# Chunk 0 of all 13 first blocks before any other chunk, other visit ranges, another root, two more raw buffers, and one background for all four modulation sums

## The chip, the cores and the metric

The kernel runs on one core of a Trainium2 chip. The metric is the device time of one execution in microseconds, the median of the runs. Before the change it is 1599.73 us (three runs, 1598.8 to 1605.01).

## What is computed

One layer of an autoregressive decoder, for 256 tokens of width 2048, all in f32. The conditioning vector c gives six modulation vectors, each silu(c) times a 2048 x 2048 part of w_ada. Two residual sub-layers follow; `mixing_sublayer` is one wide projection, three token mixers with gates, and an output projection.

```python
mod = silu(c) @ w_ada + b_ada
shift1, scale1, gate1, shift2, scale2, gate2 = split(mod, 6)
h = rms_norm(x, norm1_gain) * (1 + scale1) + shift1
x = x + gate1 * mixing_sublayer(h, w_in, ..., w_out)      # w_in: 15 blocks of 512 columns, then 3 x 2048 gates
h = rms_norm(x, norm2_gain) * (1 + scale2) + shift2
g, u = split(h @ w_ffn_in, 2)
x = x + gate2 * ((silu(g) * u) @ w_ffn_out)
```

The mixers are a stick-breaking attention, a dilated attention in three groups and a gated linear attention. Their inputs come from the first 13 blocks of w_in's columns (0 to 12).

## The kernel before

**Products.** Every f32 weight is split into two parts that TensorE takes at full pace: ACT casts the raw tile to `whi` (L167, or L245 in the Strassen pairs), and DVE subtracts to get `wlo` (L168, L231). Activations H are split likewise. A product of one 128x512 weight chunk with two row tiles of 128 tokens is six matmuls (`mm3`, lines 175 to 177; line 662 in the first stretch). `load_weights` (L142) loads two chunks at a time, 512 KB, into one of four rotating `raw` buffers (L155, L156). SP issues all loads, in the order of its own queue; a load waits until the buffer it goes to is free, and all loads behind it in the queue wait too.

**w_in.** H of chunk k (16 chunks of 128 rows) needs shift1 and scale1 of these rows. They come from column sums ("MACs"): DVE multiplies a 128x1024 tile of the transposed w_ada with silu(c), which lies broadcast in the tile "ada" (cB), and adds along the row (`column_mac`, L430). One chunk takes four MACs and four loads of 512 KB. Since not all of H is there at first, blocks 0 to 12 are visited several times: `first_chunks` does chunk 0 of blocks 1 to 4 and chunks 0 to 2 of blocks 5 to 8, then each of VISITS does a range of chunks for a group of blocks (X, Y or Z), and LAST does chunks 10 to 15 of each block. Between visits the partial sums go from PSUM to SBUF (`evict`, L623, on ACT) and are seeded again (L611, ACT). In `first_chunks` the instructions of TensorE, ACT and DVE keep the order in which they are written (`in_order`); elsewhere a scheduler with priorities (`prio`, `issue_after`) orders each engine.

**The first microseconds.** k_vec is loaded first, then x in four parts. silu(c) is spread over the partitions (16 matmuls, L379). Squares of x are summed by matmuls with ones (L549), `root_of` makes the reciprocal root (L556 to L562), and the columns of shift1 and scale1 for chunk 0 come from matmuls (`by_pe`, L705) and DVE steps (`by_dve`, L714) that meet in `part`. `keep_warm` adds matmuls that compute nothing (WARM).

**Background.** The four other vectors are also made by MACs: 128 of them, spread over the kernel by a generator that `tick` advances at state["rate"] for each two chunks. `background` (L1163) does shift2, gate1 and scale2; `gate2_bg` (L1438) is a second generator, started at the first block of w_out. `flush` at FFN unit 2 forces out all that is left.

**Later stages.** Blocks 13 and 14, the gate blocks, three gate pairs, `y_block` 0 to 3 (w_br), four blocks of w_out (the fourth in two passes, one per row tile), w_ffn_in: units 0 and 1 plain, units 2 to 10 as Strassen-like pairs (`fast_products`, L264), and w_ffn_out. `load_pair` (L218) takes its raw tile from the four `raw` buffers and from `more_raws`, which in the FFN are the tiles AR1 and "ada". The counter state["raws"] says which comes next; it is set to 0 ahead of the FFN, and only `load_pair` advances it.

Of the kernel before, what the change touches and what calls it, by code (L numbers as in the profile page):

```python
# [10 lines left out]
F32 = mybir.dt.float32  # L11
# [6 lines left out]
P = 128  # L18
# [67 lines left out]
def trunk(ctx: ExitStack, tc: tile.TileContext, I, out):  # L86
# [57 lines left out]

    def load_weights(src, k0, k1, b, spare=(), ahead=True, late=None):
# [72 lines left out]
    def load_pair(src, p, b0, b1, fast, tags):  # L218


        def raw_at(b):
            more_raws = state.get("more_raws", ())
            i = state["raws"] = (state.get("raws", -1) + 1) % (4 + len(more_raws))
            raw = S(more_raws[i], [P, 2, NB]) if i < len(more_raws) else wp.tile([P, 2, NB], F32, tag="raw", name=nm("raw"))
            nc.sync.dma_start(raw, src[b, :, 2 * p : 2 * p + 2, :])
            return raw
# [214 lines left out]
    FIRST_TAGS = ("OS0", "OS1", "OS2", "OD", "T4", "T5", "A9", "A10", "A11", "A12", "A8", "A7")  # L441
# [109 lines left out]
    def root_of(sums):  # L551


        act = nc.scalar.activation
        v, y, z, r = (x for x in S("X0", [P, 4, T]).rearrange("p a t -> a p t"))
        act(v, sums, AF.Identity, bias=eps_c[:, 0:1], scale=1.0 / D)  # L556
# [68 lines left out]
    def first_chunks():  # L625
# [37 lines left out]

        nc.sync.dma_start(vec, I["k_vec"])
        for j in range(3):
            nc.sync.dma_start(xT[j], I["x_t"][:, 4 * j : 4 * j + 4, :])
# [4 lines left out]
        for a in (0, 2):
            nc.sync.dma_start(rows[3][:, a : a + 2], I["ada_0"][:, 12 + a : 14 + a, :])
        load_two(0, 1, True)
        for b in (3, 5, 7):
            load_two(0, b)
        for k in (1, 2):
            load_mods(k)
            if k == 1:
                for b in (5, 7):
                    load_two(k, b)  # L680

        with in_order():
# [26 lines left out]
            def by_dve(k):  # L709
                row, c = rows[k // 4][:, k % 4, :], csil[:, k : k + 1]  # L710
                if k == 2:
                    nc.vector.tensor_scalar(part, row, c, None, op0=ALU.mult)
                else:
                    nc.vector.scalar_tensor_tensor(part, row, c, part, op0=ALU.mult, op1=ALU.add)  # L714

            for k in (0, 1, 4, 5, 8, 9, 12, 13):
                by_pe(rows[k // 4][:, k % 4, :], k)
            for k in (2, 3, 6, 7):
                by_dve(k)
            r = state["root"] = root_of(sums)  # L720
# [3 lines left out]
            for k in (10, 11):
                by_dve(k)
            for k in (14, 15):
                by_pe(rows[3][:, k % 4, :], k)
            by_pe(part, None, True)
# [12 lines left out]
            xs = {b: [acc_bank() if b < 3 else misc_bank([P, NB]) for _ in range(NT)] for b in BLOCKS_X}
            for b in BLOCKS_X:
                products(0, b, xs[b], True, True)
                if b % 2:
                    cast_two(0, b + 4)
                    lows(0, b + 4)
                evict(b, xs[b])
# [940 lines left out]
```

## Time and profile before

| | before |
|---|---|
| median of three runs | 1599.73 us |
| profiled execution | 1599.51 us |
| its span, first to last instruction | 1597.7 us |
| mean granted TensorE clock | 0.993 |
| TensorE busy | 1557.0 us, 97% |
| VectorE (DVE) busy | 1374.7 us, 86% |
| ScalarE (ACT) busy | 920.0 us, 58% |
| first product with w_in starts | 19.60 us |
| w_out's first product starts | 775.1 us |
| longest wait of TensorE | 13.0 us |

A row of the timeline has the start in us, the duration in us, the engine, the line of the kernel, the operation, output<-inputs, the shape and a count of like instructions drawn together; in brackets stands how long the engine was idle ahead of it and what it waited for. PE is TensorE, PEld its weight load, SPq the issue of a DMA by SyncE. A row of waits has the waiting line, the awaited line, the sum in us, the number and the longest. A row of windows has the stretch and its length, each engine's busy time with its instructions, the granted clock of TensorE (1.00 is full), the share of time in which the 16 DMA engines were busy, and GB/s. Durations of matmuls overlap; their pace is read from their starts.

### The profile page before, as it was taken

What the parts mean: (1) busy time and instruction counts of PE and PEld (TensorE: products, weight loads), DVE (VectorE), ACT (ScalarE), POOL (GpSimd) and SP (SyncE); (2) the same over time, 40 slices, a digit from 0 to 9 for tenths busy, and PEclk for the clock granted to TensorE, in tenths of its full rate; (3) what the DMA queues carried; (4) which work ended last, traced back from release to release, by engine and by line L of the source; (5) the groups of instructions that cost most, each with busy time, mean ns of one, the idle gap of its engine ahead of it and who ended that gap; (6) DMA issues with size and microseconds to landing.
All of it is one profiled execution on the core that took longest, in us unless ns stands there. A gap on an engine that the chain in (4) does not pass through costs nothing.

```text
span 1597.7 us, 20015 instructions
## 1 busy us (share of the span) xinstructions
PE 1557.0 (97%) x7067; PEld 1279.6 (80%) x7067; DVE 1374.7 (86%) x1837; ACT 920.0 (58%) x1292; POOL 5.0 (0%) x11
## 2 busy tenths in 40 slices
PE   8999999999999999999999996999999999999998
PEld 6778778888888778888887875888888888888887
DVE  7987866987978999978888876999999999789886
ACT  5787777866756454444445533555655655455553
POOL 0000000000000000000000000000000000000000
PEclk9999999999999999999999998999999999999999
DMA  9999986766787778889997784665656566656764
GB/s 349 340 335 320 353 298 215 253 189 222 256 296 272 255 245 271 295 269 333 338 332 277 262 300 140 208 212 190 201 190 213 196 196 222 201 185 188 231 205 140
DMA packets 113380, 399.20 MB, mean 250 GB/s; under 512 B 12512, under 2 KB 13408, under 8 KB 113280
## 3 DMA queue, kind: packets, MB, share of 16 engines
q1 hardware_dynamic: 112704, 395.84, 73.2%
q0 software_dynamic: 576, 2.10, 0.3%
q8 instruction: 55, 0.90, 0.2%
q14 instruction: 45, 0.37, 0.1%
HBM read 393.69 MB, written 4.19 MB: 249 GB/s over the span
## 4 chain that ended last, share of the span: by engine, by line
PE 71%; DVE 12%; DMA 8%; ACT 4%; issue 4%; SPq 0%; DVEq 0%; ACTq 0%
PE acc L176 15%; PE acc L177 14%; PE acc L175 14%; PE misc L176 8%; PE misc L177 8%; PE misc L175 8%; DVE wlo L168 3%; DMA raw<-w_ffn_in 2%; ACT whi L167 2%; DVE wlo L231 1%; DMA AR<-ada_t 1%; DVE A L231 1%; DMA raw<-w_in 1%; DMA raw<-w_out 1%; DMA raw<-w_br_gla 1%
## 5 line engine op out<-in xcount | busy, mean ns | idle before, releaser
L168 DVE TENSOR_TENSOR wlo<-raw,whi 128x1024 fp32r<-128x1024 f32 (+1 forms) x265 | 311.7, 1185 | 106.9 <-ACT whi L167 106.1
L167 ACT CAST whi<-raw 128x1024 fp32r<-128x1024 f32 (+1 forms) x265 | 269.2, 1022 | 221.5 <-PE acc L177 92.5
L176 PE MATMUL acc<-wlo,H 128*128 128x512 f32 x854 | 334.6, 392 | 4.6 <-DVE wlo L168 3.0
L175 PE MATMUL acc<-whi,H 128*128 128x512 f32 x854 | 332.0, 392 | 4.3 <-ACT whi L167 2.4
L177 PE MATMUL acc<-whi,H 128*128 128x512 f32 x854 | 333.1, 390 | 0.1
L176 PEld LDWEIGHTS acc<-wlo,H 128*128 128x128 f32 x854 | 160.5, 188 | 41.7 <-DVE wlo L168 7.8
L175 PEld LDWEIGHTS acc<-whi,H 128*128 128x128 f32 x854 | 160.4, 188 | 37.9 <-ACT whi L167 2.8
L177 PEld LDWEIGHTS acc<-whi,H 128*128 128x128 f32 x854 | 160.3, 188 | 33.3 <-DVE H L1422 0.5
L245 ACT CAST whi<-raw 128x1024 fp32r<-128x1024 f32 (+1 forms) x126 | 121.1, 973 | 63.6 <-PE acc L177 25.6
L231 DVE TENSOR_TENSOR wlo<-raw,whi 128x1024 fp32r<-128x1024 f32 (+1 forms) x126 | 139.7, 1122 | 17.6 <-ACT whi L245 16.3
L176 PE MATMUL misc<-wlo,H 128*128 128x512 f32 (+1 forms) x297 | 116.0, 390 | 1.2 <-DVE wlo L168 1.1
L177 PE MATMUL misc<-whi,H 128*128 128x512 f32 (+1 forms) x297 | 115.3, 389 | 0.0
L175 PE MATMUL misc<-whi,H 128*128 128x512 f32 (+1 forms) x297 | 113.2, 389 | 0.9 <-ACT whi L167 0.9
L177 PE MATMUL acc<-whi,A 128*128 128x512 f32 x221 | 86.2, 390 | 0.0
L176 PE MATMUL acc<-wlo,A 128*128 128x512 f32 x210 | 82.1, 391 | 2.1 <-DVE wlo L168 2.1
L175 PE MATMUL acc<-whi,A 128*128 128x512 f32 x210 | 82.0, 391 | 1.0 <-ACT whi L167 1.0
L176 PEld LDWEIGHTS misc<-wlo,H 128*128 128x128 f32 x297 | 55.8, 188 | 15.6 <-DVE wlo L168 4.0
L175 PEld LDWEIGHTS misc<-whi,H 128*128 128x128 f32 x297 | 55.7, 188 | 13.0 <-ACT whi L167 1.4
L177 PEld LDWEIGHTS misc<-whi,H 128*128 128x128 f32 x297 | 55.7, 188 | 11.5 <-DVE H L591 0.4
L231 DVE TENSOR_TENSOR A<-raw,A 128x1024 fp32r<-128x1024 f32 (+2 forms) x58 | 55.5, 962 | 3.1 <-ACT A L245 2.7
L245 ACT CAST A<-raw 128x1024 fp32r<-128x1024 f32 (+1 forms) x35 | 34.4, 989 | 31.5 <-DMA raw<-w_in 10.2
L623 ACT COPY A<-acc 128x512 f32<-128x512 f32 x64 | 37.0, 585 | 22.8 <-PE acc L177 20.1
(711 smaller groups left out, 3145.2 us busy)
## 6 DMA issues: line engine op xcount, KB each, us to landing
raw<-w_in SPq DMA_DIRECT2D x191, 512.0 KB, 5.1
raw<-w_ffn_in SPq DMA_DIRECT2D x135, 512.0 KB, 4.8
raw<-w_ffn_out SPq DMA_DIRECT2D x73, 512.0 KB, 4.3
AR<-ada_t SPq DMA_DIRECT2D x61, 512.0 KB, 5.6
raw<-w_out SPq DMA_DIRECT2D x32, 512.0 KB, 5.6
OS<-ada_t SPq DMA_DIRECT2D x26, 512.0 KB, 7.3
KD<-ada_t SPq DMA_DIRECT2D x24, 512.0 KB, 5.9
T<-ada_t SPq DMA_DIRECT2D x23, 512.0 KB, 7.5
```

Of the source, the lines that this page charges most:

```text
L167: state["cast"] = nc.scalar.copy(hi[:, :n, :], raw[:, :n, :])
L168: state["split"] = nc.vector.tensor_tensor(lo[:, :n, :], raw[:, :n, :], hi[:, :n, :].bitcast(F32), op=ALU.subtract)
L175: nc.tensor.matmul(ps, lh, rh, start=start, stop=False, skip_group_check=seeded)
L176: nc.tensor.matmul(ps, lh, rl, start=False, stop=False, skip_group_check=seeded)
L177: state["mm"] = nc.tensor.matmul(ps, ll, rh, start=False, stop=stop, skip_group_check=seeded)
L231: done = nc.vector.tensor_tensor(dst, x, y, op=ALU.subtract)
L245: nc.scalar.copy(hi[:, :n, :], src)
L623: nc.scalar.copy(A[b][:, t, :], pss[t])
```

## The change

1. In `first_chunks`, x's first quarter is loaded ahead of k_vec, and the rows of w_ada for chunk 0 between x's parts. The squares, warming matmuls and mods are interleaved in another order.
2. `root_of` drops one ACT step: Ln reads the sums directly, and DVE makes v beside it. DVE steps of `part` stand between the root's steps.
3. Chunk 0 is done for all 13 blocks first, in the order 1, 2, 3, 4, 9, 10, 11, 12, 0, 5 to 8; then chunks 1 and 2 of blocks 5 to 8. All but blocks 5 to 8 are evicted after chunk 0.
4. VISITS and LAST have other ranges: the last visits now begin at chunk 9 (X), 11 (Y) or 10 (Z).
5. `load_weights` takes X1 and X2 as two more raw buffers, from the first visit until gate_block(0, 1).
6. One background makes shift2, scale2, gate1 and gate2 in this order. It starts at the first of the last visits with rate 0.7 (before, blocks 0 to 4 there had rate 0), and later rates are lower. `gate2_bg` is gone.
7. state["raws"] starts the FFN at 1 and is also advanced by `load_weights`, which there has no extra buffers, so that each call counts in fours.
8. `normed` and the sums of h are issued behind the latest split.

```diff
-RATE_IN, RATE_MID, RATE_GATES, RATE_PAIRS, RATE_Y, RATE_LAST = 0.8, 0.6, 0.65, (0.42, 0.25, 0.25), 0.55, 0.75
+RATE_IN, RATE_MID, RATE_GATES, RATE_PAIRS, RATE_Y, RATE_LAST = 0.7, 0.6, 0.6, (0.25, 0.2, 0.2), 0.55, 0.75
-RATES_OP, RATES_FFN = (0.95, 0.9, 0.0), (0.95, 0.95, 0.85, 0.8)
+RATES_OP, RATES_FFN = (0.9, 0.7, 0.0), (0.75, 0.9, 0.7, 0.6)
-WARM = (8, 2, 1, 3)
+WARM = (8, 2, 2, 2, 2, 3)
+RATE_FIRST = 0.7
-VISITS = ((BLOCKS_Z, 0, 3, 3, 5), (BLOCKS_X, 1, 5, 5, 7), (BLOCKS_Y, 3, 6, 7, 8), (BLOCKS_Z, 3, 7, 8, 10),
-          (BLOCKS_X, 5, 10, 10, 12), (BLOCKS_Y, 6, 10, 12, 14), (BLOCKS_Z, 7, 10, 14, 16))
-LAST = (10, 16)
+VISITS = ((BLOCKS_X, 1, 4, 4, 5), (BLOCKS_Z, 1, 5, 5, 7), (BLOCKS_Y, 3, 7, 7, 9), (BLOCKS_X, 4, 9, 9, 11),
+          (BLOCKS_Y, 7, 11, 11, 13), (BLOCKS_Z, 5, 10, 13, 16))
+LAST = {b: (k0, KC) for bs, k0 in ((BLOCKS_X, 9), (BLOCKS_Y, 11), (BLOCKS_Z, 10)) for b in bs}
...
+    def raw_tile(more):
+        i = state["raws"] = (state.get("raws", -1) + 1) % (4 + len(more))
+        return S(more[i], [P, 2, NB]) if i < len(more) else wp.tile([P, 2, NB], F32, tag="raw", name=nm("raw"))
...
-                raw = wp.tile([P, step, w], F32, tag="raw", name=nm("raw"))
+                raw = raw_tile(state.get("load_raws", ()))
...
-            more_raws = state.get("more_raws", ())
-            i = state["raws"] = (state.get("raws", -1) + 1) % (4 + len(more_raws))
-            raw = S(more_raws[i], [P, 2, NB]) if i < len(more_raws) else wp.tile([P, 2, NB], F32, tag="raw", name=nm("raw"))
+            raw = raw_tile(state.get("more_raws", ()))
...
-    def root_of(sums):
+    def root_of(sums, between):
...
-        act(v, sums, AF.Identity, bias=eps_c[:, 0:1], scale=1.0 / D)
-        act(y, v, AF.Ln)
+        first = xT[0][:, 0, :]
+        act(y, sums, AF.Ln, bias=eps_c[:, 0:1], scale=1.0 / D)
+        nc.vector.tensor_scalar(v, sums, 1.0 / D, EPS, op0=ALU.mult, op1=ALU.add)
         act(y, y, AF.Exp, scale=-0.5)
         act(z, y, AF.Square)
+        between()
+        nc.vector.tensor_tensor(first, first, y, op=ALU.mult)
         nc.vector.tensor_mul(z, z, v)
         nc.vector.tensor_scalar(z, z, -0.5, 1.5, op0=ALU.mult, op1=ALU.add)
+        nc.vector.tensor_tensor(first, first, z, op=ALU.mult)
...
+        x_in(0, 0, 4)
         nc.sync.dma_start(vec, I["k_vec"])
...
+            squares(0, "X1", 0, 4, sums)
+            keep_warm(WARM[2])
+            squares(1, "X2", 0, 4, sums)
+            keep_warm(WARM[3])
+            squares(2, "AR0", 0, 4, sums)
+            on_pe(0, 1)
+            on_dve(2, 3)
+            for a in (0, 2):
+                squares(3, "AR1", a, a + 2, sums)
+            r = state["root"] = root_of(sums, lambda: on_dve(6, 7))
+            on_pe(4, 5)
+            keep_warm(WARM[4])
+            on_pe(8, 9)
             for dst, ps in state["spreads"]:
                 nc.scalar.copy(dst, ps)
-            normed(r, 0, 1)
...
+            on_dve(10, 11)
+            on_pe(12, 13)
+            by_pe(part, None)
+            on_pe(14)
+            by_pe(rows[3][:, 3, :], 15, True)
...
+    state["load_raws"] = ("X1", "X2")
...
     def background():
-        for seg in (SEG_SHIFT2, SEG_GATE1, SEG_SCALE2):
...
+        for seg in (SEG_SHIFT2, SEG_SCALE2, SEG_GATE1, SEG_GATE2):
...
+    state["rate"] = RATE_FIRST
...
+    state["load_raws"] = ()
     gate_block(0, 1, turns)
...
-    bg.append(gate2_bg())
...
-    state["raws"] = state["tiles"] = 0
+    state["raws"], state["tiles"] = 1, 0
```

Three places in the order. First SP's queue at the entry of the FFN's pairs, before: ada_t is w_ada transposed (a MAC's load), L156 a plain weight load, L225 a raw of a pair.

```order
L423 DMA A_1749_8140<-ada_t 128x1024
L423 DMA KC_8170<-ada_t 128x1024
L156 DMA raw_8234<-w_ffn_in 128x1024
L156 DMA raw_8240<-w_ffn_in 128x1024
L156 DMA raw_8246<-w_ffn_in 128x1024
...
L225 DMA raw_8449<-w_ffn_in 128x1024
L225 DMA AR_1825_8457<-w_ffn_in 128x1024
L225 DMA raw_8455<-w_ffn_in 128x1024
L225 DMA ada_8367<-w_ffn_in 128x1024
L225 DMA ada_8417<-w_ffn_in 128x1024
```

And the same place now (the lines of the new file are L426, L161 and L228):

```order
L161 DMA raw_8088<-w_ffn_in 128x1024
L426 DMA KC_7973<-ada_t 128x1024
L161 DMA raw_8094<-w_ffn_in 128x1024
L161 DMA raw_8100<-w_ffn_in 128x1024
L161 DMA raw_8106<-w_ffn_in 128x1024
L161 DMA raw_8112<-w_ffn_in 128x1024
L161 DMA raw_8234<-w_ffn_in 128x1024
L228 DMA ada_8408<-w_ffn_in 128x1024
L161 DMA raw_8240<-w_ffn_in 128x1024
```

The tile ada_8367, the first raw of the first pair, stood behind nine other raws of pairs. Now the load into "ada" stands among the plain loads, and the last load of a MAC a few rows ahead of it.

Second, DVE at the eight splits of w_out's first block (`wlo`; L1333 and L1334 are sums of the last y block, L336 a split of transposed y), before:

```order
L168 TENSOR_TENSOR wlo_6859<-raw_6856,whi_6858 128x1024
L168 TENSOR_TENSOR wlo_6865<-raw_6862,whi_6864 128x1024
L1333 TENSOR_TENSOR A_1425_6661<-A_1425_6661,acc_6756 128x512
L1333 TENSOR_TENSOR A_1425_6661<-A_1425_6661,acc_6757 128x512
L1334 TENSOR_TENSOR T_1426_6664<-T_1426_6664,A_1425_6661 128x512 x2
L168 TENSOR_TENSOR wlo_6871<-raw_6868,whi_6870 128x1024
L168 TENSOR_TENSOR wlo_6877<-raw_6874,whi_6876 128x1024
L168 TENSOR_TENSOR wlo_6883<-raw_6880,whi_6882 128x1024
L168 TENSOR_TENSOR wlo_6889<-raw_6886,whi_6888 128x1024
```

And now (L433 is a MAC, its second row the reading of the sum):

```order
L173 TENSOR_TENSOR wlo_6908<-raw_6905,whi_6907 128x1024
L173 TENSOR_TENSOR wlo_6914<-raw_6911,whi_6913 128x1024
L1426 TENSOR_TENSOR A_1425_6660<-A_1425_6660,acc_6761 128x512
L1426 TENSOR_TENSOR A_1425_6660<-A_1425_6660,acc_6762 128x512
L1427 TENSOR_TENSOR T_1426_6663<-T_1426_6663,A_1425_6660 128x512 x2
L433 ISA AR_1464_6803,gate_1961<-AR_1464_6803,ada_90,gate_1961 128x1024
L433 ISA gate_1961 128x1
L433 ISA AR_1465_6830,gate_1961<-AR_1465_6830,ada_90,vec 128x1024
L433 ISA gate_1961 128x1
L433 ISA KD_6858,gate_1961<-KD_6858,ada_90,vec 128x1024
L433 ISA gate_1961 128x1
L173 TENSOR_TENSOR wlo_6920<-raw_6917,whi_6919 128x1024
```

Three MACs of gate 2 now stand ahead of the third split; three more follow among the fourth to eighth.

Third, ACT at the first visit now (A_119 is the partial sum of block 8, L630 an evict, L618 a seed, whi_571 and whi_577 the first visit's weights, X_127 a raw in one of the added buffers):

```order
L630 COPY A_118_539<-misc_458 128x512
L618 COPY misc_605<-A_63_316 128x512
L630 COPY A_119_542<-acc_465 128x512
L630 COPY A_119_542<-acc_466 128x512
L172 CAST whi_571<-X_127_569 128x1024
L172 CAST whi_577<-X_130_575 128x512
L618 COPY misc_606<-A_63_316 128x512
L618 COPY acc_645<-A_66_327 128x512
L618 COPY acc_646<-A_66_327 128x512
L618 COPY misc_684<-A_76_354 128x512
```

Before, the first visit was block 9's (whi_476 and whi_482), which needed no seed:

```order
L167 CAST whi_476<-raw_474 128x1024
L167 CAST whi_482<-raw_480 128x512
L623 COPY A_95_457<-acc_339 128x512
L623 COPY A_95_457<-acc_340 128x512
L623 COPY A_96_460<-acc_341 128x512
L623 COPY A_96_460<-acc_342 128x512
L623 COPY A_97_463<-misc_343 128x512
L623 COPY A_97_463<-misc_344 128x512
L623 COPY A_98_466<-misc_345 128x512
L623 COPY A_98_466<-misc_346 128x512
L167 CAST whi_518<-raw_516 128x1024
```

The casts for the first visit stood ahead of the evicts of blocks 5 to 8 (A_95 to A_98); now they stand behind the last of these evicts, and the seeds of the following visits are among them.

More of the change, by code (lines that the diff above doesn't have):

```diff
@@ L476, in ada_chunks @@
             if k % 4 == 0:
-                with tc.issue_after(queue[mybir.EngineType.DVE]):
+                with tc.issue_after(state["split"].ins if "split" in state else queue[mybir.EngineType.DVE]):
                     normed(state["root"], k, k + 4)
@@ L641, in load_two, with load_one, cast_one @@
                     nc.sync.dma_start(raw, w_in[b : b + 2, :, k, :].rearrange("b p c -> p b c"))
+        def load_one(k, b):
+            raw = raws[k, b] = wp.tile([P, 2, NB], F32, tag="raw", name=nm("raw"))
+            nc.sync.dma_start(raw[:, 0, :], w_in[b, :, k, :])
+        def cast_one(k, b):
+            hi = wp.tile([P, 2, NB], F32R, tag="whi", name=nm("whi"), bufs=4)
+            lo = wp.tile([P, 2, NB], F32R, tag="wlo", name=nm("wlo"), bufs=4)
+            nc.scalar.copy(hi[:, 0], raws[k, b][:, 0])
+            parts[k, b] = hi[:, 0, :], lo[:, 0, :]
+            parts[k, b, "lows"] = [
+                lambda: nc.vector.tensor_tensor(lo[:, 0], raws[k, b][:, 0], hi[:, 0].bitcast(F32), op=ALU.subtract)
+            ]
         def cast_two(k, b, single=False):
@@ L707, in by_pe, with on_pe, on_dve @@
                     )
[L709 to L720, printed above, removed]
+            def on_pe(*ks):
+                for k in ks:
+                    by_pe(rows[k // 4][:, k % 4, :], k)
+            def on_dve(*ks):
+                for k in ks:
+                    row, c = rows[k // 4][:, k % 4, :], csil[:, k : k + 1]
+                    if k == 2:
+                        nc.vector.tensor_scalar(part, row, c, None, op0=ALU.mult)
+                    else:
+                        nc.vector.scalar_tensor_tensor(part, row, c, part, op0=ALU.mult, op1=ALU.add)
+            squares(0, "X1", 0, 4, sums)
[11 more added lines that the diff above has]
+            on_pe(8, 9)
             for dst, ps in state["spreads"]:
                 nc.scalar.copy(dst, ps)
-            normed(r, 0, 1)
[L724 to L728, printed above, removed]
+            on_dve(10, 11)
[3 more added lines that the diff above has]
+            by_pe(rows[3][:, 3, :], 15, True)
             cast_two(0, 1, True)
@@ L734, in first_chunks, with start_block, columns @@
             nc.vector.tensor_tensor(sh, mods[1], vec[:, o : o + 1], op=ALU.add)
-            keep_warm(WARM[3])
+            keep_warm(WARM[5])
             make_h(0, True)
+            banks = {}
+            def start_block(b, k=0):
+                if b not in banks:
+                    banks[b] = [misc_bank([P, NB]) if b in (3, 4, 11, 12, 6, 7) else acc_bank() for _ in range(NT)]
+                products(k, b, banks[b], k == 0, b not in BLOCKS_Y or k == TWO - 1)
+            def columns(*which):
+                for i in which:
+                    seg, half = (SEG_SCALE1, SEG_SHIFT1)[i // 2], i % 2
+                    column_mac(mod1[seg], seg, 1, half, rows[4 + i])
+                    if i == 1:
+                        scaled_gain(mod1[seg], ROW_N1, 1, 2)
@@ L737, in first_chunks @@
             lows(0, 1)
+            load_one(0, 0)
+            load_mods(1, (2, 3))
             cast_two(0, 3)
             lows(0, 3)
+            load_two(0, 5)
+            cast_two(0, 9)
+            lows(0, 9)
+            load_two(0, 7)
             normed(r, 1, 4)
[L741 to L747, printed above, removed]
@@ new lines, in first_chunks @@
+            evict(1, banks[1])
+            cast_two(0, 11)
+            lows(0, 11)
+            load_two(1, 5)
+            columns(0, 1)
+            start_block(2)
+            evict(2, banks[2])
+            start_block(3)
+            evict(3, banks[3])
+            cast_one(0, 0)
+            lows(0, 0)
+            load_two(1, 7)
+            rows.extend(S(tag, [P, HALF]) for tag in FIRST_TAGS[:4])
+            load_mods(2, range(4))
+            columns(2, 3)
+            start_block(4)
@@ L1235, in sums_of_h @@
         full = S(scratch[0], [P, 4, T])[:, c]
-        nc.vector.tensor_tensor(full, hT[0][j][:, c].bitcast(F32), hT[1][j][:, c].bitcast(F32), op=ALU.add)
+        with tc.issue_after(state["split"].ins):
+            nc.vector.tensor_tensor(full, hT[0][j][:, c].bitcast(F32), hT[1][j][:, c].bitcast(F32), op=ALU.add)
         sf = S(scratch[1], [P, 4, 2, P])[:, :, :n]
```

113 lines of the change are left out of this document (66 added, 47 removed).

## The prediction

> **What bounds the kernel now.** I read the page first, then the waits of TensorE by line, then the timeline around the largest of them and windows over the stages that the change touches.
>
> ```profile
> span 1597.7 us, 20015 instructions
> PE 1557.0 (97%) x7067; PEld 1279.6 (80%) x7067; DVE 1374.7 (86%) x1837; ACT 920.0 (58%) x1292; POOL 5.0 (0%) x11
> PE 71%; DVE 12%; DMA 8%; ACT 4%; issue 4%; SPq 0%; DVEq 0%; ACTq 0%
> L623 ACT COPY A<-acc 128x512 f32<-128x512 f32 x64 | 37.0, 585 | 22.8 <-PE acc L177 20.1
> ```
>
> TensorE is busy for 97% of the span, and the change alters no product of a weight with an activation. What it can win are TensorE's idle places and slow stretches, and what it can lose are new ones. The waits of TensorE, largest first, say how much there is:
>
> ```profile
> PE misc L175 <- ACT A L245: 13.0, 1, 13.0
> PE acc L176 <- DVE wlo L168: 5.1, 7, 1.6
> ...
> PE acc L662 <- ACT H L586: 3.1, 2, 2.2
> ```
>
> One wait of 13.0 us is larger than all others together. Its place in the timeline, just ahead of the first Strassen pairs of the FFN, with the smaller ones 28 us earlier:
>
> ```profile
> 949.23 1.04 ACT L167 CAST whi<-raw 128x1024 fp32r<-128x1024 f32 x1 [8.81 <-DMA raw<-w_ffn_in]
> 950.33 0.50 PE L175 MATMUL acc<-whi,H 128*128 128x512 f32 x1 [2.39 <-ACT whi L167]
> 951.59 0.50 PE L176 MATMUL acc<-wlo,H 128*128 128x512 f32 x1 [0.76 <-DVE wlo L168]
> ...
> 971.09 1.28 DVE L430 CUSTOM_DVE_ANT_0 KC<-KC,ada,gate 128x1024 f32<-128x1024 f32 x1
> 972.40 7.43 SPq L225 DMA_DIRECT2D ada<-w_ffn_in  x2
> 977.17 1.04 ACT L245 CAST A<-ada 128x1024 fp32r<-128x1024 f32 x1 [5.52 <-DMA ada<-w_ffn_in]
> 978.26 1.22 PE L175 MATMUL misc<-A,H 128*128 128x512 f32 x2 [12.97 <-ACT A L245]
> 980.12 0.63 PE L177 MATMUL misc<-A,H 128*128 128x512 f32 x1
> ...
> 983.83 0.40 PE L175 MATMUL misc<-A,H 128*128 128x512 f32 x1
> 984.06 0.39 PE L176 MATMUL misc<-A,H 128*128 128x512 f32 x1
> ```
>
> The tile "ada" holds silu(c), which every column MAC (L430) reads. The first raw of the first pair is to land in it. So its load waits for the last MAC of gate 2 (971.09 + 1.28), lands about 4.7 us later, is cast, and TensorE starts at 978.26. From 983.83 on the matmuls start 0.23 us apart (983.83 to 984.06); ahead of that twelve fill the 5.57 us from 978.26, where twelve at 0.23 would take 2.8. That is 2.8 more, of which I put 2.6 down to the slow pitch. A block-chunk (one 128x512 weight chunk, two row tiles, three products each) is 6 x 0.23 = 1.37 us of TensorE.
>
> **The FFN's entry: -18.** In the changed order the state of the raw buffers makes "ada" the sixth raw instead of the first, no MAC stands between the last splits of the second plain FFN block and the pairs, and 8 MACs instead of 18 stand between FFN splits. Removed: the 13.0 wait, the 2.6 of slow matmuls, and the 2.39 + 0.76 at 950 (a cast that waited for its load among MAC loads). That is 18.7. What is late next is the ordinary raw and its cast, which other buffers allow several blocks earlier; I leave 0.7 for it. Bounds: -20, if the other small wait there goes too, and -14, if the 950 waits stay and one new wait of 1 us comes.
>
> [...]
>
> **w_out: +7.** Gate 2's MACs now run in the main background, so they are among w_out's splits. In the order, 6 more MACs stand among the eight splits of w_out's first block. What DVE had to do there before:
>
> ```profile
> 774.50 2.36 DVE L168 TENSOR_TENSOR wlo<-raw,whi 128x1024 fp32r<-128x1024 f32 x2
> 776.77 1.28 DVE L1333 TENSOR_TENSOR A<-A,acc 128x512 f32<-128x512 f32 x2
> 777.97 1.28 DVE L1334 TENSOR_TENSOR T<-T,A 128x512 f32<-128x512 f32 x2
> 779.17 3.62 DVE L168 TENSOR_TENSOR wlo<-raw,whi 128x1024 fp32r<-128x1024 f32 x3
> ...
> 750.00:794.00 44.00, 43.38 (x195) 35.40 (x194) 39.58 (x52) 19.48 (x21) 0.00 (x0) 1.00 0.92 332
> ```
>
> The third split starts at 779.17 and serves the chunks that TensorE reaches two pairs (5.5 us) after the first, which it took near 775: about a microsecond of slack. Three MACs ahead of it (3 x 1.28 = 3.8) make it late by some 3 us, and the other three eat DVE's 4.4 idle microseconds in the window and add 2: +5. Blocks 1 and 2 have little more (+1). In the fourth block, run in two passes, the residual adds (lines 1477 and 1478 of the new file) bunch between its splits: +1. Bounds: +2, if the splits run ahead by then, and +13, if all 7.7 us of MACs and the loads that go with them (share of DMA already 0.92) fall on the path.
>
> **The start of w_in: +2.5 to the first product.**
>
> ```profile
> 2.84 0.22 ACT L534 ACTIVATE tiny<-vec 128x16 f32<-128x16 f32 x1 [0.83 <-DMA vec<-k_vec]
> 5.55 1.06 ACT L544 ACTIVATE X<-T 128x1024 f32<-128x1024 f32 x1 [2.50 <-DMA T<-x_t]
> 6.29 2.45 PE L379 MATMUL misc<-KC,pick 128*128 128x128 f32 x16
> 12.97 0.47 ACT L556 ACTIVATE X<-acc,eps_c 128x256 f32<-128x256 f32 x1 [1.98 <-PE acc L549]
> 19.60 0.63 PE L662 MATMUL acc<-whi,H 128*128 128x512 f32 x1
> ```
>
> The vector k_vec is now loaded behind the first half megabyte of x, so silu(c) starts nearer to 5 than at 2.84, and the 16 spread matmuls end near 10.9 instead of 6.29 + 2.45 = 8.74. In TensorE's fixed order the squares' sums, four warming matmuls and eight of mods now stand behind them: the sums are ready near 14.8 instead of 12.97, +1.8. Behind the sums the chain loses one ACT step (0.47), but `part`, which DVE now finishes between root steps, and the last two chunks of mods come behind it: I put +0.7. Bounds +1 and +3.6.
>
> **First stretch: +2.4 net.**
>
> ```profile
> 40.89 1.53 PE L662 MATMUL acc<-whi,H 128*128 128x512 f32 x4 [2.22 <-ACT H L586]
> 42.49 1.22 PE L662 MATMUL acc<-wlo,H 128*128 128x512 f32 x2
> 43.51 1.77 PE L662 MATMUL acc<-whi,H 128*128 128x512 f32 x4
> 45.12 0.63 PE L662 MATMUL acc<-wlo,H 128*128 128x512 f32 x2
> ```
>
> Before, TensorE waited 3.1 for H of chunks 1 and 2 (the two waits above), and behind the 2.22 ten matmuls took 45.12 - 40.89 = 4.23 instead of 2.3: 5.1 in all, which goes, since chunk 0 of 13 blocks is 17.8 us of cover. New: DVE has some ten splits (12 us), 8 MACs (10.2) and the residual parts of H ahead of H(2), some 25 us, against 17 block-chunks (23.3 us): 1.5. Then the first visit: ACT casts its first weights only behind the two evicts of block 8 (0.585 each), so evicts, cast (1.04) and split stand between two products: 2.6, and 0.9 for the next split. H(3), behind seeds and casts: 1.5. Slow matmuls after them: half of the 2 us above, 1.0. Sum 7.5 - 5.1.
>
> **Later visits: -3.**
>
> ```profile
> 50.00:80.00 30.00, 30.00 (x130) 23.74 (x129) 26.83 (x39) 23.99 (x39) 0.00 (x0) 1.00 1.00 378
> 160.00:200.00 40.00, 37.07 (x156) 28.28 (x155) 34.80 (x54) 29.41 (x47) 0.00 (x0) 1.00 0.97 353
> ...
> PE acc L176 <- DVE wlo L168: 2.2, 4, 1.1
> PE misc L176 <- DVE wlo L168: 1.1, 2, 0.9
> PE misc L175 <- ACT whi L167: 0.9, 1, 0.9
> ```
>
> The last three rows are the waits of 80 to 210 us: 4.2, with the DMA engines full. Two more raw buffers let loads run ahead, and the last visits, of five chunks instead of three, need fewer ada bytes for each block-chunk; I take off 3 of the 4.2. The whole of w_in is thus 2.5 + 2.4 - 3 = +2, bounds -10 and +9.
>
> **Last visits, +1; gate pairs, -2.**
>
> ```profile
> 200.00:240.00 40.00, 38.84 (x170) 31.64 (x170) 25.57 (x30) 31.93 (x72) 0.00 (x0) 1.00 0.88 298
> 240.00:280.00 40.00, 39.95 (x206) 33.20 (x205) 26.08 (x35) 30.72 (x63) 2.02 (x1) 1.00 0.63 213
> ...
> PE acc L176 <- DVE wlo L231: 1.4, 1, 1.4
> PE acc L175 <- DVE acc L282: 1.2, 1, 1.2
> ```
>
> By the order, 14 more MACs are done by the end of the last visits. They take 17.9 us of DVE, which has 28 idle in these two windows, and 14 loads of 0.52 MB at 353 GB/s, 1.49 us each, 21 us, against 0.12 x 40 + 0.37 x 40 = 20 unused: hidden but for 1 (0 to 3). In the gate pairs (the last two rows are waits of 480 to 900 us) fewer MACs stand ahead of merges and splits: -2 (-4 to +1).
>
> **Sum.** -18 + 7 + 2 + 1 - 2 = -10 on the profiled execution's 1599.51, which is within 0.3 of the median, 1599.73: 1589.5.
>
> **Rivals.** B, full cover in w_in: with two more buffers the loads run far enough ahead that no split waits; the visits' 4.2 and the new 7.5 go, w_out costs only 2. Sum: -18 + 2 + (2.5 - 5.1 - 4.2) + 1 - 2 = -23.8, so 1575.7. For it: the added buffers; against: the first visit's casts behind evicts, which the order shows.
>
> C, DVE in w_out: all six MACs and their loads on the path (+13) and w_in at its upper bound (+9): -18 + 13 + 9 + 1 - 2 = +3, 1602.5, no change. For it: DVE 39.58 of 44; against: TensorE lost only 0.6 there.
>
> A, slower: transfers become the bound. By the order 14 loads move ahead of the end of the last visits and 7 into w_out: 21 x 1.49 = 31 us, of which my sum charges 8 (1 + 7). If none is hidden: -10 + 23 = +13, 1612.5. It decides once the share of DMA in the last visits is 0.97 or more with casts that wait for raws. Against: 0.88 and 0.63. [...]
>
> D, the entry wait stays: some MAC or load of gate 2 still ends late, and the 18 are not won: +8, 1607.5.
>
> **Numbers.** A change of 0.5% is 8 us (about what can be told from none): 1591.7 and 1607.7 are the borders. Forecast 0.52 (its own range 1583 to 1597; seven in ten of it below 1591.7), B 0.22, C 0.14, A 0.07, D 0.05. Faster: 0.36 + 0.22 = 0.58; same: 0.16 + 0.14 + 0.02 = 0.32; slower: 0.07 + 0.03 = 0.10. The range goes from a little below B to C: 1574 to 1602, and leaves out A, D and the outer part of each.
>
> **What would show it.** Right: no wait above 1 us on a cast of "ada" at the first pairs; waits on wlo splits of some 5 us in w_out's first block; the first product of w_in near 22; waits of 2 to 3 us where the first visit begins. Wrong: the FFN entry keeps a wait over 5 us, or w_in up to the last visits is off from now by more than 8 us either way.

## The result: 1.7% slower, and where the time went

The changed kernel takes 1628.92 us (median of four runs, 1624.78 to 1630.94) against 1599.97 us before it (median of four as well): a ratio of 1.0167, 95% interval 1.0142 to 1.0191. The forecast was 1589.5 with a range of 1574 to 1602. Of the five terms of its sum one was right. The largest loss stands where the sum had +1, and no rival had its cause.

First the page of the changed kernel and its waits of TensorE. The new lines 180 to 182 are `mm3`, L172 and L173 the cast and split of weights, L929 the transposes of queries and keys, L1210 those of the dilated attention's mixture:

```profile
span 1629.0 us, 20083 instructions
PE 1572.1 (97%) x7072; PEld 1290.2 (79%) x7072; DVE 1377.7 (85%) x1841; ACT 934.3 (57%) x1305; POOL 4.0 (0%) x11
...
PE acc L180 <- ACT whi L172: 14.7, 8, 4.4
PE misc L1210 <- DVE T L1198: 10.0, 1, 10.0
PE acc L181 <- DVE wlo L173: 6.6, 12, 0.8
PE misc L929 <- DVE A L917: 5.0, 1, 5.0
PE misc L1499 <- DVE OS L1490: 3.1, 1, 3.1
```

The 13.0 us wait for the cast of "ada" is gone. In its place stand 14.7 for casts of weights, eight times, and two long waits on lines that waited 0.7 us at most before. DVE and ACT do as much as before, so this is no lack of engine time; something comes in the wrong order.

TensorE takes the same 6378 matmuls with streamed weights in both kernels. The n-th of them can be compared: its start now less its start before is the time lost up to that place, called the lag below. (Other matmuls lie between them, so single values within the mixers are not exact; from 1800 on both kernels have all matmuls of the mixers behind them.)

| n-th weight matmul | place | lost by then, us |
|---|---|---|
| 0 | first product of w_in | 5.4 |
| 960 | in the last visits | 9.2 |
| 1800 | first gate pair, mixers done | 36.5 |
| 2880 | last y block | 31.6 |
| 3360 | w_out's end | 51.8 |
| 3600 | plain FFN units | 51.3 |
| 3840 | first pairs of the FFN | 31.5 |
| 6360 | end | 31.3 |

So +5.4 at the start, +3.8 in the visits, +27.3 around the mixers, -4.9 from the gate pairs to the last y block, +20.2 in w_out, -19.8 at the FFN's entry. Of the last the profile after shows this, first as SP issues loads and then as a window:

```profile
961.12 0.33 SPq L426 DMA_DIRECT2D KC<-ada_t  x1
...
975.24 0.33 SPq L228 DMA_DIRECT2D ada<-w_ffn_in  x1
```

```profile
985.00:1000.00 15.00, 15.00 (x68) 12.43 (x67) 7.49 (x7) 7.12 (x8) 0.00 (x0) 1.00 0.66 202
```

The load into "ada" is issued at 975.24, right behind the last MAC (973.9 + 1.3). That is some 37 us ahead of TensorE's first matmul of a pair, which starts at 1012.63, and in the window TensorE is busy throughout at clock 1.00.

**The mixers.** Where the stick-breaking scores add a bias (L956), they need k_bias, a constant of 64 KB that is loaded into the tile KC. It is one of a block of five (k_low, k_bias, k_dist, k_lvl, w_gla_a; 32 to 512 KB a load) that all three mixers need. This is SP's issue of k_bias, before the change:

```profile
235.87 0.42 SPq L788 DMA_DIRECT2D KC<-k_bias  x1
```

And after it, with loads of MACs and weights ahead of them in the queue and the wait of DVE for k_bias:

```profile
342.91 0.33 SPq L426 DMA_DIRECT2D AR<-ada_t  x1
343.33 2.18 SPq L161 DMA_DIRECT2D raw<-w_in  x4
...
365.58 0.43 SPq L877 DMA_DIRECT2D KC<-k_bias  x1
```

```profile
371.55 0.77 DVE L956 TENSOR_TENSOR misc<-misc,KC 128x256 f32<-128x256 f32 x2 [3.65 <-DMA KC<-k_bias]
```

k_bias comes 130 us later, and the rest of the block 118 to 130 us later. The attention steps, which were interleaved with the last visits, come behind the constants and then run one upon the other. At 480 to 530 us nothing is left to lay between them:

```profile
498.26 4.41 PE L929 MATMUL misc<-ident,A 128*128 128x128 f32 x24 [5.04 <-DVE A L917]
...
519.79 1.58 PE L1210 MATMUL misc<-ident,T 128*128 128x128 f32 x5 [10.04 <-DVE T L1198]
```

The stretch of 480 to 520 us before and after (TensorE's busy time is the first number behind the length):

```profile
480.00:520.00 40.00, 40.00 (x187) 33.23 (x186) 34.92 (x48) 26.31 (x33) 0.00 (x0) 1.00 0.78 266
```

```profile
480.00:520.00 40.00, 24.80 (x120) 20.52 (x119) 27.52 (x78) 35.64 (x102) 0.00 (x0) 0.90 0.45 151
```

**w_out.** TensorE's waits of 780 to 930 us after the change, and what SP had issued ahead of the longest, 4.4:

```profile
PE acc L180 <- ACT whi L172: 8.9, 5, 4.4
PE acc L181 <- DVE wlo L173: 3.3, 6, 0.8
```

```profile
861.16 0.33 SPq L426 DMA_DIRECT2D KD<-ada_t  x1
863.57 0.33 SPq L426 DMA_DIRECT2D KC<-ada_t  x1
863.94 0.43 SPq L426 DMA_DIRECT2D H<-ada_t  x1
864.78 0.33 SPq L426 DMA_DIRECT2D A<-ada_t  x1
865.21 14.70 SPq L161 DMA_DIRECT2D raw<-w_out  x7
```

```profile
874.54 1.04 ACT L172 CAST whi<-raw 128x1024 fp32r<-128x1024 f32 x1 [9.29 <-DMA raw<-w_out]
```

A load of a MAC waits until the MAC that used its tile is done: between 855 and 866 us SP waits for MACs three times, 5.9 us in all. Meanwhile the weight loads behind it wait as well: SP issues none between 857.25 and 865.21. The one issued at 865.21, behind four MAC loads of 512 KB, lands 9.2 us later. The cast is idle for 9.29 us.

### The profile page after: what moved, and what is told of

Same layout as the page of the kernel before. It is cut to its first block, busy times and chain, and to the rows that moved or that the text cites. A ratio compares the mean times of both kernels' runs of the same rounds, so it can differ in the third digit from the quotient of the medians.

```text
span 1629.0 us, 20083 instructions
## 1 busy us (share of the span) xinstructions
PE 1572.1 (97%) x7072; PEld 1290.2 (79%) x7072; DVE 1377.7 (85%) x1841; ACT 934.3 (57%) x1305; POOL 4.0 (0%) x11
## 4 chain that ended last, share of the span: by engine, by line
PE 55%; DMA 5%; DVE 3%; issue 1%; ACT 1%; SPq 0%; ACTq 0%; DVEq 0%
PE acc L180 11%; PE acc L181 11%; PE acc L182 11%; PE misc L180 7%; PE misc L182 7%; PE misc L181 7%; DMA raw<-w_out 3%; DMA A<-x_blocks 1%; ACT whi L172 1%; DMA raw<-w_br_gla 1%; DVE wlo L173 1%; PE misc L1409 0%; PE misc L1499 0%; DVE AR L433 0%; DVE wlo L234 0%
## 5 line engine op out<-in xcount | busy, mean ns | idle before, releaser
L172 ACT CAST whi<-raw 128x1024 fp32r<-128x1024 f32 x220 | 226.0, 1034 | 218.9 <-PE acc L182 111.8
L173 DVE TENSOR_TENSOR wlo<-raw,whi 128x1024 fp32r<-128x1024 f32 x220 | 261.6, 1198 | 95.0 <-ACT whi L172 93.5
L181 PE MATMUL acc<-wlo,H 128*128 128x512 f32 (+1 forms) x856 | 336.3, 393 | 3.7 <-DVE wlo L173 3.3
L180 PE MATMUL acc<-whi,H 128*128 128x512 f32 (+1 forms) x856 | 331.6, 392 | 6.2 <-ACT whi L172 5.8
L182 PE MATMUL acc<-whi,H 128*128 128x512 f32 (+1 forms) x856 | 334.9, 391 | 0.0
L248 ACT CAST whi<-raw 128x1024 fp32r<-128x1024 f32 (+1 forms) x133 | 127.7, 976 | 67.3 <-PE acc L182 25.4
L234 DVE TENSOR_TENSOR wlo<-raw,whi 128x1024 fp32r<-128x1024 f32 (+1 forms) x133 | 147.6, 1127 | 17.3 <-ACT whi L248 16.0
L181 PE MATMUL misc<-wlo,H 128*128 128x512 f32 x285 | 111.5, 391 | 0.1
L182 PE MATMUL misc<-whi,H 128*128 128x512 f32 x285 | 110.6, 388 | 0.0
L180 PE MATMUL misc<-whi,H 128*128 128x512 f32 x285 | 109.0, 389 | 1.3 <-DVE KC L328 0.9
L173 DVE TENSOR_TENSOR wlo<-X,whi 128x1024 fp32r<-128x1024 f32 (+1 forms) x44 | 47.5, 1089 | 29.7 <-ACT whi L172 29.7
L180 PEld LDWEIGHTS misc<-whi,H 128*128 128x128 f32 x285 | 53.8, 189 | 13.3 <-DVE KC L328 1.3
L182 PEld LDWEIGHTS misc<-whi,H 128*128 128x128 f32 x285 | 53.5, 188 | 10.8
L630 ACT COPY A<-acc 128x512 f32<-128x512 f32 x66 | 37.4, 591 | 26.3 <-PE acc L182 23.5
```

Of the source, the lines that this page charges most:

```text
L172: state["cast"] = nc.scalar.copy(hi[:, :n, :], raw[:, :n, :])
L173: state["split"] = nc.vector.tensor_tensor(lo[:, :n, :], raw[:, :n, :], hi[:, :n, :].bitcast(F32), op=ALU.subtract)
L180: nc.tensor.matmul(ps, lh, rh, start=start, stop=False, skip_group_check=seeded)
L181: nc.tensor.matmul(ps, lh, rl, start=False, stop=False, skip_group_check=seeded)
L182: state["mm"] = nc.tensor.matmul(ps, ll, rh, start=False, stop=stop, skip_group_check=seeded)
L234: done = nc.vector.tensor_tensor(dst, x, y, op=ALU.subtract)
```

## Experiments

Theories on the mixers: **Q**, the constants' loads stand too far back in SP's queue; **V**, VectorE is too full with 14 more MACs; **B**, the two added raw buffers are in the mixers' way. Each ratio below is to the kernel before on the same chip.

**Constants early** (e1). The block of constants, with no other change:

```diff
-    kc = S("KC", [P, 8, P])
-    low_r, bias = S("T3", [P, P], F32R), kc[:, 1, :]
...
+    with prio():
+        kc = S("KC", [P, 8, P])
+        low_r, bias = S("T3", [P, P], F32R), kc[:, 1, :]
...
```

> The changed kernel, with the loads of the mixers' constants (k_low, k_bias, k_dist, k_lvl, w_gla_a) and the two copies made of them given the priority that weight loads have; nothing else. Theory Q (the constants' loads stand behind background and weight loads in SP's queue, the mixers start some 90 us late and bunch where TensorE has nothing else): the 27 us that the stretch from the last visits to the first gate pair lost come back, 1602 to 1609 us, and no wait of TensorE over 3 us is left between 270 and 560 us. Theory V (VectorE is too full with 14 more MACs there): the MACs are still there, 1624 to 1631.

Measured: 1604.38 us, ratio 1.0029 (1.0015 to 1.0044). That is 1.4% or 22 us off the changed kernel, and the MACs are all still there. SP's issue of k_bias and the window of 480 to 520 us:

```profile
209.72 0.42 SPq L878 DMA_DIRECT2D KC<-k_bias  x1
```

```profile
480.00:520.00 40.00, 39.20 (x178) 31.73 (x178) 34.93 (x49) 22.03 (x29) 0.00 (x0) 1.00 0.75 254
```

TensorE is busy for 39.20 of 40 us again; the longest wait between 270 and 560 us is 2.1. By the lag 6.1 us are still lost around the mixers (7.1 at the 960th matmul, 13.2 at the 1800th), 21 less than the 27.3. Q holds, V falls.

**Rate 0 in the first of the last visits** (e2):

```diff
-    state["rate"] = RATE_FIRST
```

> The changed kernel, with the background's rate left at 0 for the last visits of blocks 0 to 4, as before the change. Theory Q: the constants' loads stand about where they stood before, so the stretch's 27 us come back, less what the 10 or so MACs cost where they go to: 1603 to 1613. Theory V says the same; it is told apart by the run with the early constants. Theory B (the two added raw buffers X1 and X2 are in the mixers' way): no gain, 1625 to 1632.

Measured: 1621.39, ratio 1.0131 (1.0110 to 1.0153): outside what Q gave. By its lag the mixers are mended (6.9 us at the 1800th matmul, 0.1 at the 2880th), so with the background silent the constants come in time (k_bias at 245.24), and B falls. But the MACs that were not done there all came to w_out, which then lost 43 us. SP's queue has the MACs' loads ahead of w_out's in the first block, and a cast of ACT shows what that does:

```profile
820.29 1.04 ACT L172 CAST whi<-raw 128x1024 fp32r<-128x1024 f32 x1 [13.10 <-DMA raw<-w_out]
```

**Four raw buffers** (e3):

```diff
-    state["load_raws"] = ("X1", "X2")
```

> The changed kernel without the two added raw buffers (X1, X2) from the first visit on. Theory B (these buffers delay the mixers): 27 us come back, 1602 to 1609, plus up to 4 us of waits in the visits. Theory Q: k_bias goes up in the queue by some 60 rows but w_gla_a stays late, so the mixers still start late and most of the loss stays: 1618 to 1634.

Measured: 1628.08, ratio 1.0174 (1.0153 to 1.0194), no difference from the changed kernel. B falls a second time, and so does the gain that the forecast gave to these buffers. The run also says that k_bias alone is not the cause. It is issued at 266.98 here, 31 us later than before and not 130, and still 29 us are lost around the mixers (8.3 at the 960th matmul, 37.3 at the 1800th). What is still late is k_dist (312 and 327 us), k_lvl and w_gla_a (370 us):

```profile
266.98 0.49 SPq L876 DMA_DIRECT2D KC<-k_bias  x1
...
354.20 0.43 SPq L883 DMA_DIRECT2D T<-k_lvl  x1
...
362.83 0.51 ACT L963 CAST T<-T 128x384 fp32r<-128x384 f32 x1 [3.89 <-POOL KC L884]
```

L963 casts what comes of the attention's scores into the tile T4, in which k_lvl, the masks of the gated linear attention, lands first; the cast waits until GpSimd has read the masks there (L884). So one late constant of another mixer holds the attention up as well.

**The raw counter at 0** (e4):

```diff
-    state["raws"], state["tiles"] = 1, 0
+    state["raws"], state["tiles"] = 0, 0
```

> The changed kernel, with the raw counter at 0 instead of 1 ahead of the FFN, so that the first raw of the first pair is the tile ada again. Theory M (what took the 13 us wait away is that gate 2's MACs end earlier): no change, 1625 to 1632. Theory C (the counter took it away): a wait of 8 to 13 us for the cast of ada comes back, with the slow matmuls behind it, 1637 to 1646.

Measured: 1628.57, ratio 1.0171 (1.0145 to 1.0197), and no wait of TensorE between 950 and 1030 us. With the MACs done early, the counter does not matter: M. By the lag the FFN's entry wins 19.8 here too.

The next four start from the kernel with early constants, whose loss is w_out's. Theories: **H**, head of line, the MACs' loads hold up the weight loads in SP's queue; **L**, their bytes are too many; **D**, VectorE's time for the MACs, which was the forecast's reason.

**MAC loads by GpSimd** in w_out's first three blocks (e5):

```diff
-        return nc.sync.dma_start(raw, I["ada_t"][o : o + P, half * HALF : (half + 1) * HALF])
+        queue_of = nc.gpsimd if state.get("pool") else nc.sync
+        return queue_of.dma_start(raw, I["ada_t"][o : o + P, half * HALF : (half + 1) * HALF])
...
+    state["pool"] = True
     for n in range(3):
...
+    state.pop("pool")
```

> The kernel with early constants, in which the loads of the MACs in w_out's first three blocks are issued by GpSimd instead of SP. Theory H (w_out's loss of 20 us is head-of-line blocking: a MAC's load that waits for its tile holds the weight loads behind it in SP's queue): most of it goes, 1584 to 1592. Theory L (the bytes of these loads are too many for the DMA engines there) and theory D (VectorE's time for the MACs delays the splits): no gain, 1601 to 1608.

Measured: 1590.73, ratio 0.9924 (0.9901 to 0.9947), 1.05% or 17 us less than with early constants alone. In the order 21 MACs lie between the splits of these blocks, one more than without the edit; they are spread as 7, 7 and 7 where there were 10, 7 and 3. GpSimd issues 13 of their loads; those that fall into the first block are nearly all still SP's.

**Short MACs** (e6):

```diff
+        w = P if state.get("short") else HALF
         return nc.vector.tensor_tensor_reduce(
-            out=raw, in0=raw, in1=cB[:, half * HALF : (half + 1) * HALF], scale=1.0,
+            out=raw[:, :w], in0=raw[:, :w], in1=cB[:, half * HALF : half * HALF + w], scale=1.0,
...
+    state["short"] = True
     for n in range(3):
...
+    state.pop("short")
```

> The kernel with early constants, in which the MACs of w_out's first three blocks multiply 128 columns instead of 1024 (so these sums are incomplete); their loads are whole. Theory D: VectorE gets some 1.1 us back for each of about 17 MACs and w_out's 20 us mostly go, 1584 to 1592. Theory H: tiles come free a little earlier, 2 to 6 us off, 1598 to 1602. Theory L: no change, 1601 to 1607.

Measured: 1603.40, ratio 1.0003 (0.9990 to 1.0016), 4 us off, with intervals that touch. This kernel leaves out seven eighths of each sum that it shortens. 15 MACs, all behind the first block, take 0.35 us instead of 1.28, which frees 14 us of VectorE; w_out keeps most of its loss: D falls for the blocks that the edit reaches.

**Short MACs and short loads** (e7), with `raw[:, :c]` and c = 128 in the load as well:

> As the run with short MACs, and the loads of these MACs also bring 128 columns instead of 1024. Theory L: what the short MACs alone did not bring comes here, the sum being some 20 us: 1582 to 1589. Theory H: the loads still wait for their tiles in SP's queue, but tiles come free sooner, 1594 to 1600. Theory D: the same as with short MACs alone.

Measured: 1589.93, ratio 0.9912 (0.9885 to 0.9939), 1.2% or 19 us less than with early constants alone. That is about what L gave (some 20 us), and more than H gave (1594 to 1600). But without the bytes a load may also hold its queue and its tile for a shorter time, which was not measured, so the run does not tell the two apart; the GpSimd run does, since there all the bytes still come. TensorE's waits of 770 to 900 us, for early constants, then GpSimd loads, then short MACs:

```profile
PE acc L180 <- ACT whi L172: 8.5, 5, 3.2
PE acc L181 <- DVE wlo L173: 3.0, 6, 0.8
PE misc L1500 <- DVE OS L1491: 2.5, 1, 2.5
```

```profile
PE acc L181 <- DVE wlo L173: 3.2, 4, 1.2
PE acc L180 <- ACT whi L172: 1.3, 1, 1.3
```

```profile
PE acc L180 <- ACT whi L172: 10.3, 3, 7.9
PE acc L181 <- DVE wlo L173: 1.8, 3, 0.8
```

The wait for casts goes with the queue, not with VectorE's work. The window of 780 to 850 us with early constants, then with GpSimd loads, and SP's waits ahead of MAC loads of 780 to 880 us, in the same order:

```profile
780.00:850.00 70.00, 59.81 (x256) 45.97 (x254) 53.12 (x70) 24.20 (x30) 0.67 (x1) 0.97 0.87 306
```

```profile
780.00:850.00 70.00, 66.96 (x303) 54.18 (x302) 61.04 (x79) 30.01 (x40) 7.44 (x14) 1.00 0.95 358
```

```profile
SPq L426 <- DVE gate L433: 28.6, 14, 4.4
```

```profile
SPq L427 <- DVE gate L434: 12.4, 6, 4.7
```

The DMA engines carry 358 GB/s where they carried 306, so the bytes were not too many: L falls. One rival is left: loads on another queue might also leave the weights a larger share of the engines. The traces speak against it, since between 780 and 900 us a load of w_out takes 6.4 us from issue to landing in the median in both runs; what changes is when it is issued.

**Half the rate in w_out** (e8):

```diff
-RATES_OP, RATES_FFN = (0.9, 0.7, 0.0), (0.75, 0.9, 0.7, 0.6)
+RATES_OP, RATES_FFN = (0.45, 0.35, 0.0), (0.75, 0.9, 0.7, 0.6)
```

> The kernel with early constants and half the background's rate in w_out's first two blocks (0.45 and 0.35 instead of 0.9 and 0.7), so that some 9 MACs move on to the plain blocks of the FFN. Theories H, L and D: w_out gives back 10 to 16 us; the FFN's entry pays 2 to 5, if its raw in ada is not late: 1592 to 1599. If the entry's wait for ada depends on when the last MAC is done (as the run with the counter at 0 says), it may come back in part: up to 1606.

Measured: 1590.70, ratio 0.9922 (0.9901 to 0.9944). This is below what was expected (1592 to 1599), since the FFN pays nothing. In the order w_out's first three blocks have 14 MACs instead of 20, and the FFN 14 instead of 8. By the lag the entry of the pairs still wins 19.7 (from 10.4 at the 3600th matmul to -9.4 at the 3840th): MACs are cheap there (19.8 in the changed kernel, with 8) and dear in w_out (the table below).

Where in w_out the time is lost, as us lost by the n-th weight matmul:

| | 2952: w_out begins | 3048: one block done | 3240: three blocks done | 3336: w_out's end |
|---|---|---|---|---|
| changed kernel | 32.0 | 39.6 | 52.1 | 51.8 |
| early constants (e1) | 6.4 | 12.5 | 26.3 | 23.8 |
| GpSimd loads (e5) | 6.8 | 13.0 | 13.4 | 10.1 |
| short MACs (e6) | 8.8 | 14.3 | 25.9 | 22.2 |
| short MACs and loads (e7) | 8.2 | 15.9 | 15.9 | 11.1 |
| half rate (e8) | 3.8 | 10.7 | 14.5 | 10.3 |

In the second and third block early constants alone lose 13.8 us, and the edits change that to 0.4, 11.6, 0 and 3.8. The first block loses 5.5 to 7.7 us in all of them. These edits hardly reach it, so its cause stays open. In the changed kernel its casts wait for loads, and not for VectorE:

```profile
822.87 1.04 ACT L172 CAST whi<-raw 128x1024 fp32r<-128x1024 f32 x1 [4.37 <-DMA raw<-w_out]
```

**The start** (e9), again from early constants:

```diff
-        x_in(0, 0, 4)
         nc.sync.dma_start(vec, I["k_vec"])
+        x_in(0, 0, 4)
...
-            by_pe(part, None)
-            on_pe(14)
-            by_pe(rows[3][:, 3, :], 15, True)
+            on_pe(14, 15)
+            by_pe(part, None, True)
```

> The kernel with early constants, in which k_vec is loaded first again and the matmuls of the last two chunks of mods stand ahead of the one for part instead of behind it. Theory S (these two orders make the first product of w_in 3 to 5 us late, and the delay is carried to the end): first product near 20 to 21 us and 2 to 5 us off the whole, 1599 to 1602. Theory T (the visits are bound by transfers, so an earlier start only waits more there): first product earlier but the whole unchanged, 1602 to 1607.

Measured: 1600.47, ratio 0.9998 (0.9981 to 1.0015), 0.31% or 5 us off. The starts of the changed kernel, of the one with early constants, which has the same code there, and of this one: the 16 matmuls that spread silu(c), the root begins, the first products (and, in the first, the matmuls of part and of chunks 14 and 15 behind it).

```profile
7.71 3.51 PE L382 MATMUL misc<-KC,pick 128*128 128x128 f32 x16
...
16.36 0.47 ACT L560 ACTIVATE X<-acc,eps_c 128x256 f32<-128x256 f32 x1 [4.13 <-PE acc L552]
...
20.96 1.01 PE L730 MATMUL acc<-eps_c,T 128*128 128x1 f32 x4 [1.61 <-DVE T L744]
21.84 1.84 PE L730 MATMUL acc<-tiny,OD 128*128 128x1 f32 x8
...
24.97 1.48 PE L682 MATMUL acc<-whi,H 128*128 128x512 f32 x3
```

```profile
7.14 2.00 PE L382 MATMUL misc<-KC,pick 128*128 128x128 f32 x16
...
14.60 0.47 ACT L560 ACTIVATE X<-acc,eps_c 128x256 f32<-128x256 f32 x1 [1.62 <-PE acc L552]
...
23.21 1.91 PE L682 MATMUL acc<-whi,H 128*128 128x512 f32 x4
```

```profile
13.03 0.47 ACT L560 ACTIVATE X<-acc,eps_c 128x256 f32<-128x256 f32 x1 [1.53 <-PE acc L552]
...
19.94 1.91 PE L682 MATMUL acc<-whi,H 128*128 128x512 f32 x4
```

Against the changed kernel's profile the root begins 3.3 us earlier and the first product 5.0. But in that profile TensorE took 3.51 us for the 16 matmuls, and 2.00 for the same ones with early constants; the granted clock reads 1.00 from 4 to 12 us in both. Against the latter, from which this run starts, the root begins 1.6 us earlier and the first product 3.3; by the lag 2.9 of these are left at the end. S holds: the gain is carried to the end. The 5 us of the medians are less sure, since the intervals of the two runs, on two chips, touch.

**The counter alone, on the kernel before** (e10):

```diff
-    state["raws"] = state["tiles"] = 0
+    state["raws"], state["tiles"] = 1, 0
```

> The kernel before, with the raw counter at 1 instead of 0 ahead of the FFN, so that ada is the sixth raw of the pairs and not the first; all MACs stay where they were, the last one near 972 us. Theory M (only the early end of gate 2's MACs removes the wait): the wait moves to the third pair or stays, 1595 to 1601. Theory C (the counter alone suffices when the MACs end late, since the sixth raw is wanted some 8 us later): 10 to 16 us off, 1584 to 1591.

Measured: 1589.71, ratio 0.9932 (0.9906 to 0.9958): 0.7% faster than before with one digit. The last MAC ends at 967.2 (972.4 before), and SP issues "ada" only then; but it is now the sixth raw, ACT waits for it 2.93 us, and TensorE at most 0.67 between 950 and 1000 us.

```profile
967.23 6.54 SPq L225 DMA_DIRECT2D ada<-w_ffn_in  x2
```

```profile
970.88 0.62 ACT L245 CAST whi<-ada 128x512 fp32r<-128x512 f32 x1 [2.93 <-DMA ada<-w_ffn_in]
```

So either edit removes the wait: early MACs (e4) or the counter (this run). By the lag the counter alone wins 14.9 at the FFN's entry.

**All together** (e11): early constants, the start of e9, the rates of e8, the GpSimd loads of e5.

> All that the earlier runs point to on the changed kernel: early constants, k_vec first and part last, half the background's rate in w_out's first two blocks, and the MACs' loads there issued by GpSimd. Theory H and S together: 1590.7 of the two runs with one of the w_out edits, less 3 to 5 that the other leaves, less 2 to 5 at the start: 1581 to 1586. Theory T: 1586 to 1590.

Measured: 1583.54, ratio 0.9904 (0.9870 to 0.9938), 2.6% faster than the change as it was made and about 1% faster than the kernel before. The microseconds lie in the range of H and S together, but that is in part the chip, on which the kernel before takes 1599.5 and not 1603.1 us: the ratio is only 0.2% below that of either w_out edit (0.9924 and 0.9922), and the intervals overlap. That the edits add up is not shown.

## Why the prediction was wrong, step by step

- **FFN's entry, -18.** Right: -19.8. The text named both the counter and the early MACs as the cause; for the 13.0 us wait each alone is enough. All of the gain comes with early MACs alone (e4, -19.8), and 14.9 of it with the counter alone (e10).
- **Last visits, +1.** This step failed, and most of the miss is here. The forecast asked whether 14 more MACs and their loads fit into the idle time of VectorE and the DMA engines, and they do. It did not ask who stands behind them in SP's queue. Behind them stood constants with no priority, on which all three mixers hang: +27.3 by the lag, 22 by the run with early constants. No rival had it. Q's cause is shown by two runs that mend it in different ways, and the run with four raw buffers shows that the whole block of constants has to come in time, not k_bias alone. The order of TensorE's instructions, in which the attention's sums (L884 before, L973 now) move from behind the 1052nd full-width matmul to behind the 1421st, would have shown it beforehand.
- **w_out, +7.** The place and the sign were right, the size was a third (20.2) and the reason was wrong where most was lost. The first block, put at +5, lost 7.6; the second and third, put at +1 together, lost 12.5, and there the error lies. The 3 + 2 us were VectorE's time for the first block's six MACs; no run tests that block. Behind it VectorE's time is not the reason: the run with short MACs gives back only 4 us; what is late are weights behind MAC loads in the queue. The upper bound of +13 counted the MACs' time and their loads' bytes, not the blocking. Rival C had the place, with the same reason.
- **Start of w_in, +2.5.** +5.4 in the profile, of which some 2 go with slower spread matmuls. The squares' sums came at 16.36 where I put 14.8. But of the nine kernels with this start four have the root at 14.25 to 14.60 and the first product 2.8 to 3.6 later than before, and five, the profiled change among them, have 16.36 to 16.73 and 5.2 to 5.6: there the 16 spread matmuls took 3.00 to 3.51 us and not 2.00. So the sums were sized rightly for the faster ones; why they differ was not shown. Too small was the chain behind them, +2.0 instead of +0.7 (24.97 - 16.36 against 19.60 - 12.97; 1.5 to 2.0 in the nine): eight matmuls stood behind part and took 1.84 us, at a granted clock of 0.50 from 21 to 25 us.
- **First stretch, +2.4; later visits, -3.** The wait at the first visit was there (2.25 and 0.53 us, put at 2.6 and 0.9), and so was H(2)'s, 1.21 where I put 1.5; yet the whole stretch cost next to nothing (5.4 lost at its start, 5.6 at the 240th matmul). But the visits gained nothing: from the 240th matmul to the 960th another 3.6 us were lost, where 3 were to be won, and the buffers make no difference (e3). Why the visits lose was not tried. The whole of w_in is +9.2 where the sum had +2 and the upper bound +9, and over the 8 that the forecast named as a sign of being wrong; in the nine kernels with this start it is 5.6 to 11.3.
- **Gate pairs, -2.** -4.9 up to the last y block, -4.4 of it in the gate pairs: the right way, a little beyond the bound of -4.
- **Rivals A and D** had the direction for other causes. The DMA engines were busy for 0.88 to 0.92 of the time from 240 to 360 us, below A's 0.97, and the entry wait of D is gone.

With the constants in time the change would have come to 1604, just above the forecast's range; with w_out's queue freed as well, to 1591.

## What to carry to other kernels

Where a change puts more background loads on a queue, look at what stands behind them in that queue, the rare loads above all: a block of constants, loaded once and 118 to 130 us late, cost 22 us here, where the 14 background loads themselves had been priced at 1. That VectorE had time to spare (28 us idle before the change, for 17.9 us of MACs) said nothing of SP's queue, which issues in order: price a load by what it blocks. And read the order of the waiting engine (here TensorE's) over the whole program, not only at the places that the change names.

## What the hardware showed that was not expected

- MAC loads issued by GpSimd in place of SP (13 of them) cost 17 us less, with as many bytes.
- Behind some waits of about 2 us the granted clock fell, and behind others it did not. In the changed kernel TensorE waited 1.62 us at 190, 1.91 at 207 and 2.25 at 59 us; the stretches behind them (the granted clock is the third number from the end):

```profile
192.00:196.00 4.00, 4.00 (x19) 3.28 (x18) 3.95 (x7) 1.61 (x3) 0.00 (x0) 1.00 0.99 375
...
208.00:212.00 4.00, 3.92 (x11) 3.11 (x12) 4.00 (x7) 1.67 (x3) 0.00 (x0) 0.59 0.71 222
...
60.00:64.00 4.00, 3.58 (x10) 2.81 (x11) 4.00 (x6) 4.00 (x8) 0.00 (x0) 0.64 0.91 304
```

  The clock is 1.00 behind the first, where matmuls of 128x512 start 0.23 us apart. It is 0.59 and 0.64 behind the others (0.50 from 208 to 210 and from 62 to 64 us, where they start 0.43 apart), which so cost about 1.5 us more than the wait (an estimate from the two clocks over 4 us). What decides which wait is followed by a lower clock, no run shows.
- The start differs from run to run. In nine kernels with the same code there, the same 16 matmuls took 2.00 us in four and 3.00 to 3.51 in five, and the first product came at 22.4 to 23.2 us in the four and at 24.8 to 25.2 in the five. The granted clock does not explain all of it: from 8 to 12 us it reads 0.50 in two of the five (e4 and e6), but 1.00 in the changed kernel and with GpSimd loads (e5).
